# Attention over a cumulative-gate mask: two query blocks' scores in one PSUM bank

## The chip, the cores and the metric

One core of a Trainium2 chip runs the whole program. The metric is device microseconds of one execution, median of the runs; lower is better. The core's engines work side by side, each through its own instruction stream in order: PE (matrix multiply, into PSUM), DVE (elementwise and reductions), ACT (activation functions, copies), POOL (elementwise on SBUF) and SP (issues transfers). The kernel divides PSUM, where PE's results land, into two pools of four banks; a bank here is a tile of 128 partitions by 512 fp32 columns.

## What is computed

A small network over 512 tokens of width 1024 in fp32: a convolution/pooling block with a gated feed-forward, then two attention layers, each with a convolutional feed-forward. The change is in the first attention only:

```python
def _fox_attention(x, w_in, b_f, w_out):            # 16 heads of 64
    proj = x @ w_in                                  # q, k, v and gate logits
    c = cumsum(log_sigmoid(f_logit + b_f))           # per head, over tokens
    def block(i):                                    # 128 queries at a time
        logits = q_block @ k.T * scale + c_block[..., :, None] - c[..., None, :]
        p = softmax(where(kpos <= qpos, logits, -inf))
        return p @ v
    o = map(block, range(4))
    return merge(o) @ w_out
```

## The kernel before

The first attention is `fox` (L1112). Its loop (L1245) goes over 16 **units**, one per head. A unit is `scores(u)`, `turn(p)` and `values(u)`, and the loop is software pipelined: in pass u the program traces `scores(u + 1)`, then `values(u - 1)`, then `turn` of unit u, with `go(4)`, `go(3)` and `go(7)` between them. `go(n)` draws n steps of the query and key projections of later heads (`fast_projections`, written to the tiles `c`), about 0.3 to 0.4 us of matmuls a step. The projections run out after the eleventh unit; from then on the output projection (tiles `ta`) is the only other matmul work.

`scores(u)` goes over four query blocks qb of 128 queries; block qb sees n = 128 (qb + 1) keys. For each block:

- `qk` (L1101) takes a PSUM tile `sc` and issues three matmuls: L1107 and L1108 (the high and low part of the query against the keys, 256, 256, 384 and 512 columns wide) and L1109 (the causal mask, 128 columns).
- L1199, DVE: adds the gate row to `sc` in place and keeps the row minimum `nm`; the row has a small second instruction that reads the accumulator.
- L1201, ACT: exponential of `sc` in place, with the row sum.
- L1203 and L1204, DVE: the reciprocal of the sum, and `p` = `sc` times it, from PSUM to SBUF. This is the last use of the `sc` tile.

Below, the chain of one block from L1107 to the end of L1204 is called its **chain**.

`turn` (L1210) transposes the ten 128 x 128 blocks of `p` on PE into three PSUM tiles `ptp` (4, 3 and 3 blocks, L1215), and each is split by ACT (L183) and DVE (L185) into the SBUF tile `pT`, of which there is one. `values` (L1221) multiplies `pT` with the values into a PSUM tile `po` (eight matmuls, L1227); ACT (L1233) and DVE (L1234) take it out.

`sc`, `ptp` and `po` are drawn from one pool, `wk`, of four banks (L113); the other four banks are the pool `acc`, for `c` and `ta`. So a unit asks for eight tiles out of four banks: four `sc`, three `ptp`, one `po`. A tile gets a bank when its last user there has been released.

A framework orders the instructions of each engine at compile time, by program order among those that it takes to be ready, and adds the semaphore waits. On the chip each engine then follows that fixed order. `fast_chunk` (L493) already keeps two products in the halves of one bank (`c2[:, lo]` and `c2[:, hi]`); between them ACT copies the first half out (L519).

Of the kernel before, what the change touches and what calls it, by code (L numbers as in the profile page):

```python
# [12 lines left out]
F32 = mybir.dt.float32  # L13
# [8 lines left out]
P = 128  # L22
S = 512
# [76 lines left out]
class Net:  # L100
# [73 lines left out]
    def pool(self, *args, **kw):  # L174

        self.pooled = self.nc.gpsimd.tensor_tensor(*args, **kw)  # L176
        return self.pooled
# [920 lines left out]
            nc.sync.dma_start(out=hi[o, e].bitcast(F32), in_=(hi[r, e] if query else lo[r]).bitcast(F32))  # L1098
        return hi, lo

    def qk(self, qb, e, q, k, ib, mb):  # L1101

        n = (qb + 1) * P
        w = max(256, n)
        ps = self.wk.tile([P, S], F32, name="sc", tag="wk")
        c = slice(qb * P, n)
        self.nc.tensor.matmul(ps[:, :w], q[0][:, e, c], k[0][:, e, :w], start=True, stop=False)  # L1107
        self.nc.tensor.matmul(ps[:, :w], q[1][:, e, c], k[0][:, e, :w], start=False, stop=False)  # L1108
        self.nc.tensor.matmul(ps[:, c], ib, mb, start=False, stop=True)  # L1109
        return ps  # L1110

    def fox(self):  # L1112
        nc, tc, a = self.nc, self.tc, self.a
        with ExitStack() as es:
# [3 lines left out]
            two = pool("fox2", 2)  # L1118
# [4 lines left out]
            ib, mb = self.scores_mask(one, "mask_fox")  # L1123
# [35 lines left out]
            ps = self.wk.tile([P, S], F32, name="pf", tag="wk")  # L1159
            for k in range(KD):  # L1160
                c = slice(k * H, (k + 1) * H)
# [3 lines left out]
            e = two.tile([H, S], F32, name="fe", tag="kl", bufs=1)  # L1165
# [10 lines left out]
            qs, ks, cbs = {}, {}, {}  # L1176
# [12 lines left out]

            def scores(u):  # L1190
                j, e = divmod(u, 2)
                p = two.tile([P, 1280], F32, name="p", tag="p")
                for qb in range(NT):
                    n = (qb + 1) * P
                    pq = p[:, po_[qb]:po_[qb] + n]
                    sc = self.qk(qb, e, qs[j], ks[j], ib, mb)
                    nm = self.sm.tile([P, 1], F32, name="nm", tag="nm")
                    sc = sc[:, :n]
                    nc.vector.tensor_tensor_reduce(sc, sc, cbs[j][:, e, :n], 1.0, 3e38, ALU.add, ALU.min, nm)  # L1199
                    sm = self.sm.tile([P, 1], F32, name="se", tag="se")  # L1200
                    nc.scalar.activation(sc, sc, AF.Exp, bias=nm, scale=-1.0, accum_out=sm)  # L1201
                    r = self.sm.tile([P, 1], F32, name="re", tag="re")
                    nc.vector.reciprocal(r, sm)  # L1203
                    nc.vector.tensor_scalar(pq, sc, r, None, op0=ALU.mult)  # L1204
                return p
# [36 lines left out]
            self.low = nc.gpsimd  # L1242
            go(16)
            p = scores(0)
            for u in range(16):  # L1245
                nxt = scores(u + 1) if u < 15 else None
                go(4)
                if u:
                    values(u - 1)
                go(3)  # L1250
                turn(p)
                go(7)
                p = nxt
# [309 lines left out]
```

## Time and profile before

| | |
|---|---|
| median of 3 runs | 1773.06 us (1767.25 to 1775.32) |
| the profiled execution | 1772.77 us, of which 1770.8 us is the span from the first to the last instruction |
| PE busy | 1668.4 us, 94% |
| DVE busy | 1446.9 us, 82% |
| ACT busy | 1010.3 us, 57% |
| POOL busy | 785.3 us, 44% |

The profile is of one execution. "Busy" counts the time in which an engine had an instruction in flight; PE's matmuls overlap each other. The sixteen units of the first attention lie between 607.78 us (first score matmul) and about 773 us.

### The profile page before, as it was taken

How to read it: one execution, taken by the hardware profiler on the slowest of the kernel's cores; microseconds unless marked ns; L12 is line 12 of the kernel's file. 1: busy time of each engine (PE TensorE's matmuls, PEld its weight loads, DVE VectorE, ACT ScalarE, POOL GpSimd, SP SyncE). 2: the span in 40 equal slices, each digit the busy share in tenths (PEclk: the TensorE clock that was granted, in tenths of full speed). 3: DMA queues.
4: the chain of work that ended last, by engine and by line, in shares of the span. 5: the costliest groups of instructions: out<-in, count | busy, mean ns of one | idle time of the engine just before them, and what ended most of it. 6: DMA issues, size and time to landing. Idle time of an engine off the chain costs nothing. (4 is left out here: it accounts for less than half of the span.)

```text
span 1770.8 us, 28075 instructions
## 1 busy us (share of the span) xinstructions
PE 1668.4 (94%) x10432; PEld 1481.3 (84%) x10432; DVE 1446.9 (82%) x2207; ACT 1010.3 (57%) x1733; POOL 785.3 (44%) x528
## 2 busy tenths in 40 slices
PE   6977999999999999989999998999998999999996
PEld 6856999999787888879999987787776799999875
DVE  5985677668876788967999899855888679998999
ACT  6662444455563677645666564644667455655653
POOL 2485643330023375217565527344232185565582
PEclk9988999999999999999999999999999999999999
DMA  6469566668978664844566689797443235666653
GB/s 233 170 186 246 155 162 180 190 180 291 346 214 216 171 159 133 215 110 136 156 179 181 175 278 344 213 238 192 118 117 91 90 103 162 183 189 185 198 177 107
DMA packets 106072, 326.05 MB, mean 184 GB/s; under 512 B 9888, under 2 KB 10016, under 8 KB 93904
## 3 DMA queue, kind: packets, MB, share of 16 engines
q1 hardware_dynamic: 73088, 215.53, 35.5%
q0 software_dynamic: 25648, 73.54, 22.2%
q10 hardware_dynamic: 7200, 35.20, 5.5%
q8 instruction: 82, 1.34, 0.3%
q14 instruction: 54, 0.44, 0.1%
HBM read 274.91 MB, written 73.43 MB: 197 GB/s over the span
## 5 line engine op out<-in xcount | busy, mean ns | idle before, releaser
L183 ACT ACTIVATE wh<-raw 128x1024 fp32r<-128x1024 f32 x457 | 450.7, 997 | 403.8 <-PE c L437 91.3
L185 DVE TENSOR_TENSOR wl<-raw,wh 128x1024 fp32r<-128x1024 f32 (+1 forms) x415 | 531.1, 1294 | 132.4 <-ACT wh L183 128.8
L176 POOL TENSOR_TENSOR raw<-raw 128x512 f32<-128x512 f32 x124 | 184.4, 1487 | 247.7 <-DMA raw<-raw 203.2
L436 PE MATMUL c<-xh,wh 128*128 128x256 f32 x992 | 283.8, 286 | 10.3 <-ACT m L519 10.1
L437 PE MATMUL c<-xl,wh 128*128 128x256 f32 x992 | 282.4, 285 | 0.0
L438 PE MATMUL c<-xh,wl 128*128 128x256 f32 x992 | 281.6, 284 | 0.0
L436 PEld LDWEIGHTS c<-xh,wh 128*128 128x128 f32 x992 | 190.5, 192 | 13.0 <-ACT m L519 12.7
L437 PEld LDWEIGHTS c<-xl,wh 128*128 128x128 f32 x992 | 190.7, 192 | 0.2
L438 PEld LDWEIGHTS c<-xh,wl 128*128 128x128 f32 x992 | 190.5, 192 | 0.0
L438 PE MATMUL dn<-wh,hl 128*128 128x512 f32 x462 | 181.0, 393 | 8.6 <-DVE hl L185 8.5
L437 PE MATMUL dn<-wl,hh 128*128 128x512 f32 x462 | 181.4, 394 | 2.0 <-DVE wl L185 1.9
L436 PE MATMUL dn<-wh,hh 128*128 128x512 f32 x462 | 179.1, 394 | 0.2
L150 POOL COPY paced<-wh 128x1 f32<-128x1 f32 x48 | 36.7, 765 | 230.4 <-ACT wh L183 230.3
L176 POOL TENSOR_TENSOR wl<-raw,wh 128x1024 fp32r<-128x1024 f32 (+1 forms) x42 | 96.3, 2306 | 88.4 <-ACT wh L183 85.1
L436 PE MATMUL fa<-xh,wh 128*128 128x256 f32 (+1 forms) x400 | 133.2, 333 | 1.6 <-ACT wh L183 1.6
L437 PE MATMUL fa<-xl,wh 128*128 128x256 f32 (+1 forms) x400 | 132.7, 332 | 1.1 <-DVE xl L185 1.1
L438 PE MATMUL fa<-xh,wl 128*128 128x256 f32 (+1 forms) x400 | 132.5, 331 | 0.8 <-DVE wl L185 0.8
L176 POOL TENSOR_TENSOR rs_r<-rs_t,mhalf 128x1 f32<-128x1 f32 (+1 forms) x40 | 32.2, 806 | 193.6 <-DVE rs_t L326 193.6
L176 POOL TENSOR_TENSOR hT<-hT,tv 128x512 f32<-128x512 f32 x44 | 100.1, 2274 | 36.3 <-DVE tv L1004 29.0
L438 PEld LDWEIGHTS dn<-wh,hl 128*128 128x128 f32 x462 | 87.6, 190 | 28.2 <-DVE hl L185 10.3
L437 PEld LDWEIGHTS dn<-wl,hh 128*128 128x128 f32 x462 | 87.6, 190 | 22.5 <-DVE wl L185 4.8
L274 POOL DMA_DIRECT2D raw<-raw x62 | 74.2, 1196 | 70.9 <-DVE wl L185 21.0
(305 smaller groups left out, 4611.8 us busy)
## 6 DMA issues: line engine op xcount, KB each, us to landing
raw<-in_w_conv_dram SPq DMA_DIRECT2D x36, 1024.0 KB, 4.9
mixed<-in_narrow_dram ACTq DMA_DIRECT2D x48, 704.0 KB, 6.2
raw<-raw POOLq DMA_DIRECT2D x62, 512.0 KB, 5.1
raw<-mixed SPq DMA_DIRECT2D x51, 512.0 KB, 6.0
raw<-in_narrow_dram SPq DMA_DIRECT2D x48, 512.0 KB, 5.4
raw<-in_w_ffn_dram SPq DMA_DIRECT2D x18, 1024.0 KB, 4.8
mixed<-in_narrow_dram POOLq DMA_DIRECT2D x24, 704.0 KB, 10.2
mixed<-mixed POOLq DMA_DIRECT2D x24, 704.0 KB, 9.8
```

What stands on the lines that cost most here:

```text
L150: paced = self.nc.gpsimd.tensor_copy(m, self.ready[-1][0][:, 0:1].bitcast(F32))
L176: self.pooled = self.nc.gpsimd.tensor_tensor(*args, **kw)
L183: self.copied = self.nc.scalar.activation(hi, src, AF.Copy)
L185: return self.copied, sub(lo, src, hi.bitcast(F32), op=ALU.subtract)
L274: self.nc.gpsimd.dma_start(out=raw[:, 0:4:2, :], in_=raw[:, 1:4:2, :], accum_op=ALU.add)
L436: mm(ps, lh, rh, start=first, stop=False)
L437: mm(ps, lh, rl, start=False, stop=False)
L438: mm(ps, ll, rh, start=False, stop=last)
```

## The change

`qk` gets an argument `beside`. For qb = 1 the scores go into columns 256 to 511 of the bank that qb = 0 was given; the tile of its own is not asked for. Its first matmul is issued without `start` (`start=first`), so it does not begin the bank's accumulation anew. The `qk` call of the second attention passes no `beside` and is as it was.

```diff
-    def qk(self, qb, e, q, k, ib, mb):
+    def qk(self, qb, e, q, k, ib, mb, beside=None):
         n = (qb + 1) * P
         w = max(256, n)
-        ps = self.wk.tile([P, S], F32, name="sc", tag="wk")
+        first = beside is None
+        ps = self.wk.tile([P, S], F32, name="sc", tag="wk") if first else beside
+        o, kw = (0, {}) if first else (256, dict(skip_group_check=True))
         c = slice(qb * P, n)
-        self.nc.tensor.matmul(ps[:, :w], q[0][:, e, c], k[0][:, e, :w], start=True, stop=False)
-        self.nc.tensor.matmul(ps[:, :w], q[1][:, e, c], k[0][:, e, :w], start=False, stop=False)
-        self.nc.tensor.matmul(ps[:, c], ib, mb, start=False, stop=True)
+        self.nc.tensor.matmul(ps[:, o:o + w], q[0][:, e, c], k[0][:, e, :w], start=first, stop=False, **kw)
+        self.nc.tensor.matmul(ps[:, o:o + w], q[1][:, e, c], k[0][:, e, :w], start=False, stop=False, **kw)
+        self.nc.tensor.matmul(ps[:, o + qb * P:o + n], ib, mb, start=False, stop=True, **kw)
         return ps
...
             def scores(u):
                 j, e = divmod(u, 2)
-                p = two.tile([P, 1280], F32, name="p", tag="p")
+                p, bank = two.tile([P, 1280], F32, name="p", tag="p"), None
                 for qb in range(NT):
                     n = (qb + 1) * P
                     pq = p[:, po_[qb]:po_[qb] + n]
-                    sc = self.qk(qb, e, qs[j], ks[j], ib, mb)
+                    bank = self.qk(qb, e, qs[j], ks[j], ib, mb, bank if qb == 1 else None)
+                    sc = bank[:, 256:] if qb == 1 else bank
```

## Rows read from the trace of the kernel before

**Rows 1.** The page's head and its first part: busy time by engine.
```profile
span 1770.8 us, 28075 instructions
PE 1668.4 (94%) x10432; PEld 1481.3 (84%) x10432; DVE 1446.9 (82%) x2207; ACT 1010.3 (57%) x1733; POOL 785.3 (44%) x528
```

**Rows 2.** Stages: start:end, length, busy of PE, PEld, DVE, ACT, POOL, PEclk, DMA, GB/s.
```profile
607.78:664.80 57.02, 53.52 (x411) 48.77 (x410) 48.74 (x142) 45.09 (x102) 40.95 (x24) 1.00 0.63 159
664.80:718.69 53.89, 51.00 (x381) 46.47 (x380) 45.87 (x129) 39.76 (x90) 27.96 (x17) 0.97 0.48 134
718.69:753.94 35.25, 34.68 (x200) 28.10 (x198) 32.39 (x90) 22.76 (x57) 3.49 (x8) 1.00 0.88 231
753.94:773.00 19.06, 13.44 (x69) 10.99 (x70) 13.81 (x32) 10.25 (x23) 1.57 (x3) 0.91 0.49 121
```

**Rows 3.** PE's waits, 607 to 773 us: total, times, longest.
```profile
PE po L1227 <- DVE re L1203: 3.6, 2, 2.3
PE ptp L1215 <- DVE p L1204: 2.5, 1, 2.5
...
PE sc L1107 <- DVE pT L185: 1.8, 2, 1.6
PE ptp L1215 <- DVE o L1234: 1.0, 2, 0.5
...
PE ptp L1215 <- DVE re L1203: 0.5, 1, 0.5
```

**Rows 4.** Timeline of PE around the last unit's scores: start, length, instruction, [idle before].
```profile
753.29 0.55 PE L1215 MATMUL ptp<-ident,p 128*128 128x128 f32 x3 [0.47 <-DVE o L1234]
753.94 0.39 PE L1107 MATMUL sc<-kh,qh 128*128 128x256 f32 x1
...
756.11 0.39 PE L1107 MATMUL sc<-kh,qh 128*128 128x256 f32 x1 [1.59 <-DVE pT L185]
...
757.61 0.23 PE L1109 MATMUL sc<-mb,ib 128*128 128x128 bf16 x1
759.17 1.19 PE L1227 MATMUL po<-pT,va 128*128 128x512 f32 x2 [1.32 <-DVE re L1203]
```

**Rows 5.** Timeline of DVE, the same stretch.
```profile
752.55 0.68 DVE L1234 TENSOR_TENSOR o<-po,o 64x512 f32<-64x512 f32 x1 [0.68 <-ACT o L1233]
753.15 0.73 DVE L1204 TENSOR_SCALAR p<-sc,re 128x512 f32<-128x512 f32 x1
755.37 1.62 DVE L185 TENSOR_TENSOR pT<-ptp,pT 128x512 fp32r<-128x512 f32 x3 [1.48 <-ACT pT L183]
...
758.68 0.34 DVE L1204 TENSOR_SCALAR p<-sc,re 128x128 f32<-128x128 f32 x1
```

**Rows 6.** Timeline: first unit's first matmul; chains of qb = 0, longest and shortest.
```profile
607.78 0.28 PE L1107 MATMUL sc<-kh,qh 128*128 128x256 f32 x1
...
664.80 0.28 PE L1107 MATMUL sc<-kh,qh 128*128 128x256 f32 x1
671.89 0.35 DVE L1204 TENSOR_SCALAR p<-sc,re 128x128 f32<-128x128 f32 x1
...
737.25 0.28 PE L1107 MATMUL sc<-kh,qh 128*128 128x256 f32 x1
740.50 0.35 DVE L1204 TENSOR_SCALAR p<-sc,re 128x128 f32<-128x128 f32 x1
```

**Rows 7.** Line L519: its instructions and who waited for it.
```profile
L519 ACT ACTIVATE m<-c x62: 357/385/390, 238.4 to 1640.8; 128x256 f32<-128x256 f32 x62
...
  PE c L436: 10.1, 9
```

**Rows 8.** One long stop of PE, and the stage behind it (columns as in Rows 2).
```profile
678.56 0.52 PE L1215 MATMUL ptp<-ident,p 128*128 128x128 f32 x3 [2.48 <-DVE p L1204]
...
680.00:700.00 20.00, 20.00 (x147) 18.33 (x146) 17.72 (x51) 14.76 (x36) 11.01 (x6) 0.91 0.43 119
```

## Prediction

> **What bounds the kernel now.** I read the page's first part, then the stages around the change, then who PE waits for there, and last the timeline of single units. PE is busy for 94% of the span and DVE for 82% [rows 1], so over the whole kernel PE sets the time, and only time in which PE stands still can be won. The reader should take from the stages how little of that there is where the change acts. The first attention runs from 607.78 to about 773 us. PE is busy in 53.52 + 51.00 + 34.68 + 13.44 = 152.6 of these 165.2 us, so it stands still for 12.6 us; DVE works 48.74 + 45.87 + 32.39 + 13.81 = 140.8 us, which is 85% [rows 2]. Two engines are near full, each in a fixed order. In the stage before the last PE is full (34.68 of 35.25 us); in the last, where projections and most of the output projection have run out, it is 13.44 of 19.06.
>
> PE's waits name five groups of 9.4 us together [rows 3]. The timeline shows what four of them are: a new tile that waits for a bank. In the last unit the first score matmul starts at 753.94 us, right after the 512-wide normalisation of the unit before ended (753.15 + 0.73 = 753.88); the second stands 1.59 us until `pT` has been read out of the transposes' banks; `po` stands 1.32 us until the 128-wide normalisation has ended (758.68 + 0.34 = 759.02), although its inputs were split by 755.37 + 1.62 = 756.99; the third transpose tile stands 0.47 us for the copy-out of `po` (752.55 + 0.68 = 753.23) [rows 4, 5]. The "reciprocal" that the wait table names for `po` is thus the neighbour of the normalisation that frees the bank. So bank waits are 3.6 (`po`) + 1.8 (`sc`) + 1.0 + 0.5 (`ptp`) = 6.9 us. The fifth, 2.5 us, is a transpose that waits for its data [rows 3].
>
> **The change part by part.** *What is the same.* No instruction is added or dropped: three matmuls, the DVE and ACT steps of qb = 1 keep their shapes and counts, and no transfer or POOL instruction moves. An offset of 256 columns changes no duration that I can see a reason for; I cost it at nothing.
>
> *What is removed.* Each of the 16 units asks for seven tiles instead of eight, and while the scores are alive they hold three banks, not four. In the last unit the three transposes' banks are still held until 756.11 us, so the one that waited 1.59 us there would only be another score tile (qb = 2): the 1.8 us of `sc` waits stay. But `po` no longer has to wait for a normalisation of the same unit: in the last unit a bank is free at 756.99, before the last score matmul at 757.61 [rows 4, 5]. So the 3.6 us go, and the 1.5 us of `ptp` with them: **5.1 us** gained at most by this way. The bounds are nothing (the bank is free but PE's order does not use it sooner) and 6.9 us.
>
> *What is added.* In the program qb = 1's matmuls come after the whole chain of qb = 0, and they now write into a tile which DVE and ACT have still to use. The columns are disjoint, so the question is whether that is a wait. The trace has the same case in `fast_chunk`: a product into one half of `c2` waits for ACT's copy out of the other half (L519): 10.1 us over 9 of 62 such places, on PE, although no data passes between the halves [rows 7]. So L1107 of qb = 1 will wait for L1204 of qb = 0. The Trainium skill says the same and says why: its page "PSUM — Partial Sum Buffer", section "PSUM bank collisions raise a hardware error", has the rule to guard PSUM by bank and quadrant of partitions, not by address, since two engines on one bank collide even at disjoint columns. This is the rule that speaks against the change; by a guard on addresses alone there would be no new wait and the sum would be 2.6 us lower; the trace agrees with the rule.
>
> The new wait is long by itself. From the first matmul to the end of the normalisation, the chain of qb = 0 takes 740.50 + 0.35 - 737.25 = 3.6 us at the shortest, 671.89 + 0.35 - 664.80 = 7.4 us at the longest, and 759.02 - 753.94 = 5.1 us in the last unit [rows 4 to 6]. Queued behind the waiting matmul on PE are whatever was ordered after it: projection or output-projection matmuls, the other scores, `po`, the transposes. DVE's L1199 and ACT's L1201 of qb = 1 wait for it, and DVE's order behind them. What covers it is that the order is made at compile time with the wait known: qb = 2 and 3 and the steps of the projections can be put ahead of it. Units follow at (753.94 - 607.78) / 15 = 9.74 us [rows 4, 6], so there is a unit's worth of other matmuls for it, up to the last units. What remains is the time by which DVE is later on the chip than the order took it to be. Bounds: 0 if the cover holds in all units (not less: a wait gives nothing back); at the other end each unit stops PE as long as its longest stop here, 2.48 us [rows 8], 16 x 2.48 = 40 us. The nearest row is the half-bank wait of L519, 10.1 / 62 = 0.16 us a place; I take it for 16 places: **2.6 us**. If the cover is gone, a stop costs more than itself: behind the one of 2.48 us the 20 us stage shows a granted clock of 0.91 (between the levels 1.2 and 2.4 GHz), that is 0.09 x 20 / 0.5 = 3.6 us at the lower level, some 1.8 us lost [rows 8].
>
> *The sum*, against the profiled execution: 1772.77 - 5.1 + 2.6 = 1770.3 us. The median of the runs shown is 0.3 us above the profiled one, so I forecast **1770.5 us**, a gain of 0.15%. About 0.5% (8.9 us) is what a measurement of this kernel can tell from no change, so this is "the same".
>
> **The rivals.** *Slower: two chains in series become the pace.* Its place is the bank that qb = 0 and 1 share: it is held for both chains. With the mean of the three chains above, (3.6 + 5.1 + 7.4) / 3 = 5.4 us, two take 10.8 us. It decides from the point where two chains outlast the 9.74 us between units; here by 1.06 us. Over 15 intervals that is 16 us: 1772.8 + 16 = 1789 us. For it: the longest chain alone is 7.4 us, and DVE at 85% makes each of the three DVE steps of a chain queue. Against: turning `p` comes a pass after its scores, so a late qb = 1 has a pass of slack, and the shortest two chains take only 7.2 us.
>
> *Faster: the free bank lets PE fill.* If banks were all that held PE, its 12.6 us of standing still in the attention would go [rows 2]: 1772.8 - 12.6 = 1760 us. For it: four of five named waits are for banks. Against: 2.5 us are a data wait, 1.8 us stay as shown, and in the last stage, which has 5.6 of the 12.6 us [rows 2], the projections have run out and PE hangs on the last units' chains.
>
> *Nothing: the change doesn't do what it says.* The bank is free, but DVE, which makes what `po` and the transposes need, is late by as much, so PE stops at the same places on data; or the new wait takes just what the bank gave. 1773 us. For it: DVE's 85%.
>
> **How the numbers follow.** Forecast 0.45, slower 0.20, faster 0.15, nothing 0.20. The forecast's own range is 1766 (6.9 gained, nothing paid) to 1775 (nothing gained, 2.6 paid). Runs of one kernel lie 4 us to either side besides, so forecast and nothing together reach from about 1764 to 1779. I take 1763 to 1784: below, it goes toward the faster rival; above, two thirds of the way to the slower one, which takes in a milder form of it. This leaves out less than 2 in 10. Beyond 0.5% means under 1764.2 or over 1781.9 us: faster 0.15 (that rival), slower 0.20 (that rival), same 0.65.
>
> **What would show it.** In the profile after, PE's waits should list L1107 of `sc` waiting for DVE's L1204 (or its neighbour L1203), at most some 3 us together; `po` waiting for L1203 should be gone or small; the timeline should show, per unit, the second 256-wide L1107 after the first 128-wide L1204 and after the 384 and 512 wide ones, not before. Busy times should stay: PE 1668, DVE 1447 us. Units should follow at 9.4 to 9.7 us; at 10.5 or more the slower rival holds. I am wrong if PE's stops on the new wait come to more than 5 us, if the clock falls in more of these stages than now, or if the second chain of a unit delays its transposes.

## The result and the profile after

The changed kernel takes 1785.76 us (median of 6 runs, 1781.66 to 1788.30) against 1770.77 us of the kernel before in as many runs: 1.0078 times, 95% interval 1.0060 to 1.0096. It is slower by 14 us as the ratio has it (the medians differ by 15). The forecast was 1770.5 us and the range ended at 1784.

The profiled execution took 1784.76 us, its span is 12.2 us longer than before (1783.0 against 1770.8). The page's head and first part:

```profile
span 1783.0 us, 28027 instructions
PE 1678.6 (94%) x10432; PEld 1488.4 (83%) x10432; DVE 1443.2 (81%) x2207; ACT 1009.0 (57%) x1733; POOL 741.9 (42%) x528
```

The counts are those of [rows 1], but PE is busy for 10.2 us more with the same matmuls. Three lines shift in the listing: in the changed kernel the score matmuls are L1110, L1111 and L1112 (L1107 to L1109 before), the gate step is L1204 (L1199), the exponential L1206 (L1201), reciprocal and normalisation L1208 and L1209 (L1203 and L1204), the transposes L1220, `po` L1232, its copy-out L1239. Below, "gate step" is the DVE instruction that adds the gate row to a block's scores.

The stages, from the first score matmul to the point that answers to 773.00 us before (the output projection's first matmul after the last unit, 784.24 us here and 772.67 before, and 0.33 us more). Columns are as in [rows 2]; the first boundary is the sixth unit's start here and the seventh's there, so only the last two stages can be set side by side:

```profile
607.12:660.57 53.45, 49.62 (x365) 44.46 (x363) 41.44 (x120) 38.02 (x86) 36.20 (x21) 0.97 0.60 155
660.57:725.34 64.77, 62.22 (x456) 56.09 (x456) 57.50 (x154) 48.03 (x108) 34.47 (x22) 1.00 0.57 164
725.34:764.56 39.22, 33.25 (x168) 25.57 (x168) 32.64 (x90) 23.15 (x58) 4.46 (x7) 0.91 0.71 185
764.56:784.57 20.01, 15.23 (x69) 11.94 (x70) 12.05 (x30) 8.59 (x20) 0.56 (x1) 0.83 0.09 28
```

These stages are 177.45 us long, 12.2 us more than the 165.22 us of [rows 2]: the whole loss lies in the first attention. PE stands still for 177.45 - 160.32 = 17.1 us in it, 4.5 us more than before; the other 7.7 us are busy time. Part of that is the clock. The granted clock is 0.97, 1.00, 0.91 and 0.83, so 0.03 x 53.45 + 0.09 x 39.22 + 0.17 x 20.01 = 8.5 us of full speed were not granted; by [rows 2] it was 0.03 x 53.89 + 0.09 x 19.06 = 3.3 us. (This is an estimate of what the time at the lower of the two levels, 1.2 and 2.4 GHz, took; it costs something only where PE had work.) The first score matmuls of the units lie at 607.12 us for the first and 764.56 us for the last, so units follow at 157.44 / 15 = 10.50 us, against 9.74 us before.

PE's waits in these stages, columns as in [rows 3]:

```profile
PE sc L1110 <- DVE pT L185: 3.7, 3, 2.6
PE ptp L1220 <- DVE re L1208: 3.5, 2, 2.8
PE ptp L1220 <- ACT sc L1206: 2.6, 1, 2.6
...
PE ptp L1220 <- DVE pT L185: 1.6, 1, 1.6
PE sc L1110 <- DVE p L1209: 1.2, 3, 0.6
PE ptp L1220 <- DVE o L1239: 0.8, 1, 0.8
```

`po` no longer waits: the 3.6 us of [rows 3] are gone, as forecast. The new wait of block 1's matmul (`sc`) on block 0's normalisation (`p`) is the line of 1.2 us, less than the 2.6 us that I had put down. What grew are the transposes' waits, and the score tiles' wait for the transposes' banks.

Part of that is one old stop at a new place. In the kernel before, the longest of `po`'s stops began on ACT: its fixed order had a weight's first part (`wh`, L183) ahead of block 0's exponential, and that stood for POOL (L176). ACT stood so for 3.84 us before and 3.23 us in the changed kernel, and PE then stood 2.32 us for `po` before and 2.60 us for a score tile after. The first two lines are of the kernel before, the other two of the changed one:

```profile
638.16 1.06 ACT L183 ACTIVATE wh<-raw 128x1024 fp32r<-128x1024 f32 x1 [3.84 <-POOL raw L176]
640.82 1.53 PE L1227 MATMUL po<-pT,va 128*128 128x512 f32 x8 [2.32 <-DVE re L1203]
...
636.42 1.06 ACT L183 ACTIVATE wh<-raw 128x1024 fp32r<-128x1024 f32 x1 [3.23 <-POOL raw L176]
638.74 0.46 PE L1110 MATMUL sc<-kh,qh 128*128 128x384 f32 x1 [2.60 <-DVE pT L185]
```

The rest DVE's waits explain; the first two lines are of the kernel before, 607 to 773 us:

```profile
DVE o L1234 <- ACT o L1233: 4.9, 6, 1.8
DVE sc L1199 <- PE sc L1109: 1.0, 3, 0.7
```

and the next two of the changed kernel, 607 to 785 us:

```profile
DVE sc L1204 <- PE sc L1112: 9.2, 10, 2.3
DVE o L1239 <- ACT o L1238: 8.6, 6, 3.0
```

DVE waited for score matmuls for 1.0 us before and for 9.2 us now. One unit shows how. First PE, then DVE, in the changed kernel (start, length, instruction, idle before):

```profile
725.34 0.39 PE L1110 MATMUL sc<-kh,qh 128*128 128x256 f32 x1 [0.29 <-DVE p L1209]
...
726.46 0.23 PE L1112 MATMUL sc<-mb,ib 128*128 128x128 bf16 x1
...
727.05 0.23 PE L1112 MATMUL sc<-mb,ib 128*128 128x128 bf16 x1
727.09 1.53 PE L1232 MATMUL po<-pT,va 128*128 128x512 f32 x8
728.46 0.28 PE L1110 MATMUL sc<-kh,qh 128*128 128x256 f32 x1
...
731.76 1.09 PE L1220 MATMUL ptp<-ident,p 128*128 128x128 f32 x4 [2.83 <-DVE re L1208]
```

```profile
727.72 0.16 DVE L1208 RECIPROCAL re<-se 128x1 f32<-128x1 f32 x1 [0.58 <-ACT sc L1206]
727.92 0.35 DVE L1209 TENSOR_SCALAR p<-sc,re 128x128 f32<-128x128 f32 x1
728.97 0.43 DVE L1204 CUSTOM_DVE_ANT_0 sc<-sc,row 128x256 f32<-128x256 f32 x1 [0.70 <-PE sc L1112]
...
729.32 0.60 DVE L1204 CUSTOM_DVE_ANT_0 sc<-sc,row 128x384 f32<-128x384 f32 x1
...
729.84 0.73 DVE L1204 CUSTOM_DVE_ANT_0 sc<-sc,row 128x512 f32<-128x512 f32 x1
...
731.15 0.47 DVE L1209 TENSOR_SCALAR p<-sc,re 128x256 f32<-128x256 f32 x1
```

Blocks 2 and 3 had their scores at 726.46 + 0.23 = 726.69 and at 727.28 us. Their gate steps began at 729.32 and 729.84, right behind that of block 1, which stood 0.70 us for matmuls that started only at 728.46: after block 0's normalisation (727.92 + 0.35 = 728.27), and on PE behind `po`'s eight. So two ready steps stood 2.6 us in DVE's order behind one that was not. Their three banks and `po`'s were then held at least until the first normalisation after it ended (731.15 + 0.47 = 731.62); the transposes, which need a bank, stood 2.83 us on PE until 731.76. In all 16 units of the changed kernel the gate steps of blocks 2 and 3 follow that of block 1 in this way.

The two engines' orders disagree. In the kernel before, the score matmuls and the gate steps both go 0, 1, 2, 3 in every unit. In the changed kernel PE's matmuls go 0, 2, 3, 1 in 15 of the 16 units (0, 2, 1, 3 in the first), but DVE's gate steps and ACT's exponentials still go 0, 1, 2, 3 in all. So from a block's first score matmul to its gate step it is 4.81 us for block 2 and 4.42 us for block 3 in the mean of the units, against 1.45 and 2.13 us before.

This gives a theory that the prediction did not have. **Theory H (head of line):** the loss is that of the work which DVE's fixed order has behind block 1's gate step. The rival is the recorded one, **theory S (serial):** two chains in the shared bank outlast a unit. The recorded rival came to 1789 us, and theory H was made from the trace of the changed kernel, so its time cannot choose between them.

### The profile page after: what moved, and what is told of

It reads as the page before. It is cut to its first block, busy times and chain, and to the rows that moved or that the text cites. A ratio compares the mean times of both kernels' runs of the same rounds, so it can differ in the third digit from the quotient of the medians.

```text
span 1783.0 us, 28027 instructions
## 1 busy us (share of the span) xinstructions
PE 1678.6 (94%) x10432; PEld 1488.4 (83%) x10432; DVE 1443.2 (81%) x2207; ACT 1009.0 (57%) x1733; POOL 741.9 (42%) x528
## 5 line engine op out<-in xcount | busy, mean ns | idle before, releaser
L183 ACT ACTIVATE wh<-raw 128x1024 fp32r<-128x1024 f32 x457 | 450.8, 998 | 398.3 <-PE c L437 100.3
L185 DVE TENSOR_TENSOR wl<-raw,wh 128x1024 fp32r<-128x1024 f32 (+1 forms) x415 | 520.1, 1267 | 130.3 <-ACT wh L183 126.7
L176 POOL TENSOR_TENSOR raw<-raw 128x512 f32<-128x512 f32 x124 | 180.1, 1452 | 244.4 <-DMA raw<-raw 205.8
L176 POOL TENSOR_TENSOR wl<-raw,wh 128x1024 fp32r<-128x1024 f32 (+1 forms) x42 | 95.2, 2284 | 88.9 <-ACT wh L183 77.6
L176 POOL TENSOR_TENSOR rs_r<-rs_t,mhalf 128x1 f32<-128x1 f32 (+1 forms) x40 | 33.2, 831 | 193.0 <-DVE rs_t L326 191.5
L176 POOL TENSOR_TENSOR hT<-hT,tv 128x512 f32<-128x512 f32 x44 | 86.1, 1956 | 41.9 <-DVE tv L1004 41.9
```

The costliest lines, as they stand in the source:

```text
L183: self.copied = self.nc.scalar.activation(hi, src, AF.Copy)
L185: return self.copied, sub(lo, src, hi.bitcast(F32), op=ALU.subtract)
```

## The experiments

The ratios are to the kernel before, run beside each, with 95% intervals.

**The waiting block last.** The order of the blocks is the only change (the other lines keep block 0's bank for block 1); the bank stays shared and block 1 still waits for block 0.

```diff
-                for qb in range(NT):
+                for qb in (0, 2, 3, 1):
...
-                    bank = self.qk(qb, e, qs[j], ks[j], ib, mb, bank if qb == 1 else None)
-                    sc = bank[:, 256:] if qb == 1 else bank
+                    tile_ = self.qk(qb, e, qs[j], ks[j], ib, mb, bank if qb == 1 else None)
+                    if qb == 0:
+                        bank = tile_
+                    sc = tile_[:, 256:] if qb == 1 else tile_
```

> The changed kernel with the query blocks of a unit gone through in the order 0, 2, 3, 1 instead of 0, 1, 2, 3; the bank is still shared by 0 and 1, so block 1's matmuls still wait for block 0's normalisation. Theory H (head of line: in DVE's fixed order block 1's gate step stands ahead of those of blocks 2 and 3, so DVE stops for it with ready work behind): DVE's waits for the score matmuls in the attention fall from 9.2 us to under 3 us and the time falls to 1770 to 1776 us. Theory S (serial: the bank is held for two chains in a row, whatever DVE's order): two chains are as long as before, the units stay at 10.3 us or more, 1782 to 1792 us.

Measured: 1775.04 us, 1.0018 (1.0003 to 1.0032). Its timeline for one unit, PE and then DVE, and DVE's wait for score matmuls in the attention (here the gate step is L1206, the normalisation L1211):

```profile
738.49 0.36 PE L1110 MATMUL sc<-kh,qh 128*128 128x256 f32 x1
...
739.76 0.23 PE L1112 MATMUL sc<-mb,ib 128*128 128x128 bf16 x1
...
740.35 0.23 PE L1112 MATMUL sc<-mb,ib 128*128 128x128 bf16 x1
...
743.59 0.28 PE L1110 MATMUL sc<-kh,qh 128*128 128x256 f32 x1
```

```profile
740.10 0.29 DVE L1206 CUSTOM_DVE_ANT_0 sc<-sc,row 128x128 f32<-128x128 f32 x1
...
740.31 0.60 DVE L1206 CUSTOM_DVE_ANT_0 sc<-sc,row 128x384 f32<-128x384 f32 x1
...
740.82 0.73 DVE L1206 CUSTOM_DVE_ANT_0 sc<-sc,row 128x512 f32<-128x512 f32 x1
...
745.10 0.42 DVE L1206 CUSTOM_DVE_ANT_0 sc<-sc,row 128x256 f32<-128x256 f32 x1
```

```profile
DVE sc L1206 <- PE sc L1112: 1.7, 1, 1.7
```

Blocks 2 and 3 go through at once (740.31 and 740.82); block 1's matmuls come at 743.59, 5.1 us after block 0's, and its gate step 6.6 us after block 0's first matmul. The bank is held longer than in the changed kernel (over the 16 units, from block 0's first matmul to block 1's gate step: 7.10 us in the mean against 5.99), and yet units follow at 9.74 us again. To the end of block 1's normalisation, where the bank comes free, it is 9.97 us against 8.69, and 8.69 is under the 9.74 us between units before, so theory S's condition is not met in the mean even in the changed kernel. Theory S falls: a longer hold and hardly any loss. Theory H's numbers hold. PE's score matmuls go 0, 2, 3, 1 here in all units, as in 15 of 16 of the changed kernel; what differs is DVE's and ACT's order. From its first score matmul to its gate step block 2 now takes 1.88 us and block 3 1.83 us in the mean.

**That order without sharing.** The kernel before, with only the line `for qb in (0, 2, 3, 1)` changed.

> The kernel before with the blocks in the order 0, 2, 3, 1 and no bank shared: the price of that order alone. Theories H and S both: no wait is added, 1769 to 1775 us, the same as before. If the order of the blocks matters by itself (a third theory: any change of order costs), over 1780 us.

Measured: 1776.11 us, 1.0017 (1.0002 to 1.0032). The order costs 0.17% by itself, just clear of nothing and 1.1 us above what both theories gave. So with the order 0, 2, 3, 1 sharing the bank adds 0.01% net. Whether the freed bank brings nothing and the wait costs nothing, or the two cancel, this pair does not show; its intervals leave some 0.2% (4 us) open.

**One block behind the wait instead of two.** As the first experiment, with the order 0, 2, 1, 3.

> The changed kernel with the blocks of a unit in the order 0, 2, 1, 3; bank shared by 0 and 1. One gate step (block 3's) is now queued behind block 1's wait on DVE, against two in the changed kernel and none with the order 0, 2, 3, 1. Theory H (head of line): between those two, 1776 to 1782 us. Theory S (the bank is held for two chains): as the changed kernel, 1783 us or more, or, if the later start of chain 1 alone were what mattered, no better than that.

Measured: 1778.34 us, 1.0043 (1.0027 to 1.0058), between the two, as theory H has it, though its interval reaches into that of the first experiment. On DVE block 2's step now comes before the wait and block 3's right after it:

```profile
737.65 0.60 DVE L1206 CUSTOM_DVE_ANT_0 sc<-sc,row 128x384 f32<-128x384 f32 x1
...
742.73 0.41 DVE L1206 CUSTOM_DVE_ANT_0 sc<-sc,row 128x256 f32<-128x256 f32 x1
...
743.07 0.72 DVE L1206 CUSTOM_DVE_ANT_0 sc<-sc,row 128x512 f32<-128x512 f32 x1
```

From its first score matmul to its gate step block 2 takes 1.87 us in the mean and block 3 4.66 us. But the time itself is weak support. The profiled execution is the slowest of the six (1783.97 us), DVE stands only 1.7 us for score matmuls in it, and its longest stop is again ACT's for POOL, 7.33 us, behind which PE stood 6.99 us:

```profile
643.13 1.06 ACT L183 ACTIVATE wh<-raw 128x1024 fp32r<-128x1024 f32 x1 [7.33 <-POOL raw L176]
645.21 0.80 PE L1110 MATMUL sc<-kh,qh 128*128 128x512 f32 x1 [6.99 <-DVE pT L185]
```

The runs with the order 0, 2, 3, 1 have this stop of PE at 4.8 to 5.1 us. Whether the order of the blocks makes it longer is not shown.

**The wait alone.** The kernel before, four tiles and nothing shared, with an edge that makes block 1's first matmul wait for block 0's normalisation (`scaled`); the lines that name these two instructions are left out.

```diff
...
+                    if qb == 1:
+                        tc.add_manual_dep(self.opened.ins, scaled.ins.name, mybir.DependencyInfo(mybir.DependencyClass.Sync, mybir.DependencyReason.DATA), reason="wait")
```

> The kernel before, each block in a bank of its own, with one edge added: block 1's first matmul waits for block 0's normalisation. No bank is freed and none is shared, so the wait is measured by itself. Theory H and theory S: the wait is the whole cause, 1782 to 1792 us, DVE's waits for score matmuls 6 us or more. If sharing the bank itself were the cause (or the wait cost only its 2.6 us as forecast), 1770 to 1776 us.

Measured: 1798.58 us, 1.0141 (1.0118 to 1.0163), above all that was expected. The trace shows a difference: here PE's order too has blocks 2 and 3 behind the waiting matmul, in all 16 units. One unit of PE, and PE's wait there over the attention (L1206 is the normalisation in this listing):

```profile
752.91 0.28 PE L1107 MATMUL sc<-kh,qh 128*128 128x256 f32 x1
...
757.61 0.36 PE L1107 MATMUL sc<-kh,qh 128*128 128x256 f32 x1 [2.56 <-DVE p L1206]
...
757.96 0.42 PE L1107 MATMUL sc<-kh,qh 128*128 128x384 f32 x1
...
758.44 0.47 PE L1107 MATMUL sc<-kh,qh 128*128 128x512 f32 x1
```

```profile
PE sc L1107 <- DVE p L1206: 11.8, 5, 2.6
```

So the wait is enough for the loss without any sharing. That it costs more than in the changed kernel because PE's order too has ready work behind it is my reading; the kernels differ in the bank as well, and no run takes the two apart.

**The wait alone, the waiting block last.** The same edge with the order 0, 2, 3, 1.

> Four banks' worth of score tiles as before (none shared), order 0, 2, 3, 1, and the added edge from block 0's normalisation to block 1's first matmul. With the order 0, 1, 2, 3 this edge cost 1.4%. Theory H: with nothing queued behind it the same edge costs little, 1772 to 1780 us. Theory S, and any theory by which the length of two chains is what costs: 1790 us or more, as with the other order.

Measured: 1777.32 us, 1.0035 (1.0016 to 1.0054). The same edge that cost 1.41% costs 0.35%, of which 0.17% is the order's. Sharing the bank in this order came to 0.18%; the intervals overlap, so that the freed bank is worth 0.17% here is neither shown nor excluded.

**Both blocks' matmuls first.** The matmuls of blocks 0 and 1 one after the other into their halves, then their steps in turn.

```diff
...
+                bank = self.qk(0, e, qs[j], ks[j], ib, mb)
+                self.qk(1, e, qs[j], ks[j], ib, mb, bank)
+                for _ in zip(block(0, bank), block(1, bank[:, 256:])):
+                    pass
+                for qb in (2, 3):
+                    for _ in block(qb, self.qk(qb, e, qs[j], ks[j], ib, mb)):
+                        pass
```

Here `block` makes the steps of `scores` for one block, and stops after the gate step, after the exponential and at the end.

> The changed kernel, but the matmuls of blocks 0 and 1 are issued one after the other into their halves and the steps of both blocks alternate (gate step 0, gate step 1, exponential 0, exponential 1, then the two reciprocals and normalisations): the bank is shared and PE waits for neither, while DVE and ACT still take turns on it. Theory H: the new wait on PE and DVE is gone, and only the gain of the freed bank is left, 1766 to 1772 us. Theory S: the bank is now held for one chain and a half, most of the loss goes, 1772 to 1778 us. If a freed bank brings nothing and the halves of one bank cost by themselves, 1780 us or more.

Measured: 1777.89 us, 1.0029 (1.0015 to 1.0043). Block 1's matmuls follow block 0's at once, and the loss is a third of the change's. But theory H gave 1766 to 1772 us for this, and missed; the time lies in the range that theory S gave. So 0.29% stays that neither the new wait nor DVE's order behind it accounts for. In this form DVE and ACT take turns on the bank, which the run does not separate from the rest.

**Where the loss sits.** `and u < 11`, or `and u >= 11`, is added to the condition that shares the bank.

> The bank is shared in units 0 to 10 only (projections still run beside them); units 11 to 15 have a tile for each block. If the cost comes with each unit, 11/16 of 14 us: 1780 to 1783 us. If it sits where PE has no other matmuls, under 1776 us.

> The bank is shared in units 11 to 15 only. If the cost comes with each unit, 5/16 of 14 us: 1775 to 1778 us. If it sits where PE has no other matmuls, 1779 us or more.

Measured: 1777.93 us, 1.0033 (1.0015 to 1.0052) with units 0 to 10 shared, and 1778.53 us, 1.0033 (1.0014 to 1.0051) with units 11 to 15. The two add up to 0.66% of the 0.78%. By unit it is 0.03% in the first eleven and 0.07% in the last five, where the projections have run out; the intervals overlap, so that a unit costs more there is not shown. The first lies under its expectation for a cost by unit and the second just above; neither place has it all.

Together, with the mean over the 16 units of the time from block 0's first matmul to the gate steps of blocks 1, 2 and 3 (differences of starts in the timelines):

| kernel | order | block 1, us | block 2, us | block 3, us | units at, us | ratio |
|---|---|---|---|---|---|---|
| before | 0 1 2 3 | 2.99 | 3.79 | 5.15 | 9.74 | 1 |
| changed | 0 1 2 3 | 5.99 | 6.35 | 6.90 | 10.50 | 1.0078 |
| shared, third | 0 2 1 3 | 6.79 | 3.10 | 7.28 | 10.19 | 1.0043 |
| shared, last | 0 2 3 1 | 7.10 | 3.10 | 4.03 | 9.74 | 1.0018 |
| order alone | 0 2 3 1 | 5.27 | 2.98 | 4.03 | 9.94 | 1.0017 |
| wait alone | 0 1 2 3 | 5.62 | 6.21 | 6.85 | 11.04 | 1.0141 |
| wait alone, last | 0 2 3 1 | 6.31 | 3.23 | 4.18 | 10.15 | 1.0035 |
| both matmuls first | 0 1 2 3 | 3.35 | 4.11 | 5.04 | 10.04 | 1.0029 |

Among the kernels with a shared bank or a wait, block 1's delay does not order the ratios: with the waiting block last it is longest, and the loss is small. The delay of blocks 2 and 3 sets apart the three kernels that lose 0.43% and more, in which at least one of the two is over 6 us; in the others both are at most 5.15 us and the loss is 0.35% or less. Within the two groups it does not order them: wait alone has slightly shorter delays than the changed kernel and loses nearly twice as much. The column of the units is of one execution each and holds PE's stop behind POOL, whose length differs (2.32 us before, 6.99 us with the order 0, 2, 1, 3).

## Why the prediction was wrong

- **That the halves of a bank wait for each other** was right. Block 1's matmuls came after the end of block 0's normalisation in all 16 units, by 0.05 us at the least, as the rule that I weighed has it.
- **The added wait, 2.6 us: this is the step that failed.** I sized it by what the matmul itself would stop PE, and on PE it was small (1.2 us over three stops), for the reason that I gave: blocks 2 and 3 were put ahead of the waiting matmul, on PE, in 15 of 16 units. But I took that cover for the whole wait. I named DVE's order behind it and gave it no price, and DVE's order was not changed: block 1's gate step stands ahead of those of blocks 2 and 3 in all units. On DVE the wait for scores rose from 1.0 to 9.2 us, with two ready gate steps behind it in each unit, and from there the normalisations, the banks and the transposes were late. The runs with the waiting block last show that it was what stands behind the wait, not its length; that this is DVE's queue rests on PE's score matmuls having the same order in the changed kernel (in 15 of 16 units) and in the first of these runs; ACT's order changed together with DVE's. Measured by itself, the wait cost 1.41%, some 25 us against the 2.6 us, but there with PE's order behind it too. The Trainium skill's page "PSUM — Partial Sum Buffer", section "Engine vs sequencer instructions", says that the queue of VectorE is strictly first in, first out; the unit at 725 us agrees: block 2, ready at 726.69, waited until 729.32.
- **The gain, 5.1 us,** did not come. `po`'s 3.6 us went as I said, but 2.32 of them began with ACT's stop for POOL and came back as 2.60 us at a score tile: I had read the end of that wait, the bank, and not its start. The transposes' waits, of which I took 1.5 us away, rose from 4.0 us to 3.5 + 2.6 + 1.6 + 0.8 = 8.5 us. What a freed bank is worth without the wait wasn't shown by any run: with the order 0, 2, 3, 1 bank and wait together come to 0.01%.
- **The clock behind a stop** was named with its price, but as something that happens only if the cover is gone. Three of four stages have a granted clock under 1, against two before, which was one of my signs of being wrong, and PE's busy time rose by 10.2 us. No run took the clock's share apart from the stops that led to it.
- **The rival "two chains in series"** had nearly the right time (1789 us; units at 10.5 us as its sign) for the wrong reason. The bank was held longer with the waiting block last, and the units were back at 9.74 us. Its sign was one that theory H gives too, so it could not tell the two apart; the order of DVE's steps could. Theory H does not explain everything: 0.29% was lost with both blocks' matmuls first, where it gave no loss.
- **The range** ended 1.8 us too low. It followed from the chances, in which only one mechanism, at 0.20, ended on the slower side.
- **Two readings were off.** PE's waits are not five groups of 9.4 us: the trace lists ten of 12.7 us, among them 1.8 us of the output projection for ACT (the line below), so bank waits were 6.9 of 12.7 us. And 1766 to 1775 us with 4 us to either side reaches from 1762 us, not 1764. Neither changes the forecast.

```profile
PE ta L436 <- ACT va L183: 1.8, 1, 1.8
```

No run beat the kernel before.

## To carry to other kernels

Where a change adds a wait, list for every engine in the chain what its fixed order has behind the waiting instruction, and whether that is ready; price the ready work that will stand, not only the stop of the engine that gets the new semaphore. The orders can differ: here PE's had moved the waiting block to the end and DVE's had not. If two steps must share a buffer, put the one that has to wait after the independent work in program order: here this took back 0.6 of the 0.78%. And before a wait for a bank is counted as gain, follow it back to where it began: here the longest one began on another engine, and when the bank was free it stood at another tile.

## What was not expected of the hardware

One wait edge between two engines in each of 16 units, on 1772 us, cost 1.41% when it stood ahead of two ready blocks on PE and DVE and 0.35%, the changed order included, when it stood behind them. And more than half of the 12.2 us that the changed kernel's stages are longer is not time in which PE stood still (4.5 us) but time in which it was busy with the same matmuls (7.7 us), at a granted clock of 0.83 and 0.91 in the last two stages.
